# Two edits of a two-layer diffusion backbone: square sums of 512 tokens moved to TensorE, final scalings re-ordered behind evictions and roots

## The chip, the cores and the metric

The kernel runs on one core of one Trainium2 chip, as a single launch. The metric is the device time of that launch in microseconds (us). Each core has five engines with instruction queues of their own, worked off in order: TensorE (PE, matmuls into PSUM), VectorE (DVE), ScalarE (ACT), GpSimd (POOL) and SyncE (SP, which here only issues DMAs). [...]

## The reference, cut to what matters

The program is a backbone of two layers over 1024 latent tokens and a prefix of 256 context tokens, all with 1024 features, in float32. Layer 0 mixes tokens by two groups of attention heads (A: global, B: within 128 tokens, with a sink), layer 1 by a convolution (C) and by attention over a 2-D neighbourhood (D). Before each layer the stream is normalised, and the output is a last normalisation of the latent stream:

```python
def rms_norm(x, g):
    xf = x.astype(jnp.float32)
    y = xf * lax.rsqrt(jnp.mean(xf * xf, axis=-1, keepdims=True) + EPS)
    return (y * g.astype(jnp.float32)).astype(x.dtype)
...
    for i in range(DEPTH):
        ...
        h_lat = rms_norm(x_lat, norm_g[i]) * (1.0 + sc_l[:, None, :]) + sh_l[:, None, :]
        h_ctx = rms_norm(x_ctx, norm_g[i]) * (1.0 + sc_c) + sh_c
        ...
        x_lat = x_lat + g_l[:, None, :] * y_lat
        ...
    return rms_norm(x_lat, final_g)
```

So each normalisation needs, for every token, the sum of the squares of its 1024 features, then a root, then a scaling of all features. The change touches two of these: the one that opens layer 1, for the middle 512 of the 1280 tokens, and the last one.

## The kernel before

Features lie on the 128 partitions, in 8 slices `e` (or `dk`), and tokens along the free axis, in three chunks: chunk 0 is the 256 context tokens, chunks 1 and 2 are 512 latent tokens each. A float32 product is made of three matmuls on split operands (`mm3`, L345 to L347: high by high, low by high, high by low); the split of a tile into a high part (a cast on ACT) and a low part (a subtraction on POOL or DVE) is the helper `split` (L325, L328).

**Layer 0** runs attention in 40 groups (4 head groups by 10 blocks of 128 queries). A group goes through up to 10 tiles of keys. For each tile PE makes scores `st` (L522, L526; two PSUM banks), ACT the exponential `pf` (L534) and its high part `ph`, POOL the low part `pl` (L328), and three tiles later PE adds `ov` (L473 to L475; one bank). At a group's end DVE transposes and inverts the sums (L483 to L486) and scales (`y`, L683, L685). A group's maxima for the shift are found two groups ahead: PE makes scores once more into `mx` (L633, L645; two banks), DVE reduces each (`mp`, L635, L646) and all of them to `nmt` (L429); PE transposes that (`trn`, L450), and DVE writes it into `QL` (L451), without which the group's scores can't be finished.

Other work is woven between: generators `main` (attention) and `fill` are advanced in turns, and a scheduler that knows priorities then sets each engine's order. Beside the last head group the fill is `final_proj(1)` and `norm_h(1)`: for each slice `e` the output projection of chunk 1 (`po` on PE), the eviction with residual (`x`, DVE, L967), the square (ACT, L992 and L998) and its addition into one accumulator `acc` (L1000; DVE for even `e`, POOL for odd). The squares from the second on share a single buffer, `sq1` with `bufs=1`. Then `rstd_steps` sums `acc` over partitions on PE (`trs`, L262), takes the root with a power on POOL (L247) and a Newton step on DVE (L248 to L250), and spreads it (`bc`, L273); `make_h` scales the eight slices on DVE (L335) and splits them (ACT L338, L341; DVE L339; POOL L328). Chunk 2 and chunk 0 follow once attention is done.

**The end of the program** normalises three pieces, `k` = 0 (512 tokens), 1 and 2 (256 each), in the order `EVS = "e1 a1 e2 b1 a2 f0 f1 b2 f2"`: `e` is the last projection with its evictions (L1440), squares (L1470) and sums (`sum4`, L280: four squares at once, each into its own 32 partitions of a bank `pb`), `a` and `b` are the two halves of the root (`roots` keeps for each root the DVE instruction that starts it, the POOL power and the last Newton instruction), and `f` is the scaling `final_norm`: for the slices in `FNP[k]` on ACT and POOL (L1494, L1498), for the others on DVE (L1508). After every second slice SP issues a DMA to the output (L1510). `tc.issue_after(ins)` pins the instructions of a block behind `ins`, but only those that run on the engine of `ins`; the rest of the block gets no such edge.

## Time and profile before

| what | us |
|---|---|
| median of 3 runs (lowest, highest) | 1542.24 (1541.05, 1546.29) |
| the profiled execution, whole | 1542.41 |
| its span, first to last instruction | 1540.6 |
| PE, DVE, ACT, POOL busy in the span | 1457.2, 1042.5, 746.1, 793.3 |

Times in the profile count from the start of the span. The last head group with the work woven beside it runs from about 840 to 918, and the end of the program (the pieces 1 and 2) from about 1510 to 1540.6. A row of the timeline gives start, duration, engine, line, operation, tiles and count, and in brackets how long the engine was idle before and what ended that. PEclk is the share of its full clock that TensorE was granted.

### The profile page before, as it was taken

The numbers are of one execution on the slowest core, as the hardware profiler recorded it, in microseconds if no ns is written. First come the engines' busy times: TensorE is split into PE (matmuls) and PEld (weight loads), VectorE is DVE, ScalarE is ACT, GpSimd is POOL, SyncE is SP. The second block draws the span as 40 slices with busy tenths as digits, with TensorE's granted clock in tenths as the row PEclk, the third lists the DMA queues.
The fourth block names the chain that finished last, engine by engine and source line by source line (L and its number), as shares of the span: only waits on it lengthen the run. The fifth ranks groups of instructions, "written<-read, shape, count | busy, mean of one in ns | idle before, by whom it ended". The sixth has DMA issues, their size and how long they took to land.

```text
span 1540.6 us, 21500 instructions
## 1 busy us (share of the span) xinstructions
PE 1457.2 (95%) x7112; PEld 1171.6 (76%) x7112; DVE 1042.5 (68%) x2106; ACT 746.1 (48%) x1416; POOL 793.3 (51%) x631
## 2 busy tenths in 40 slices
PE   6899999998998999999999889999999999989996
PEld 2776888796896777886776558888887788868875
DVE  2833466479678956556667948999938675567866
ACT  3721434444444455447546665443434455455564
POOL 3440335446355757557646665665533434364664
PEclk7899999999999999999999889999999999999998
DMA  9474315423312236121111112211484677877642
GB/s 367 151 243 145 103 62 175 147 64 93 120 56 71 89 124 225 52 69 53 42 43 58 44 33 79 59 56 41 141 258 143 204 214 225 261 225 235 186 125 109
DMA packets 154168, 199.83 MB, mean 130 GB/s; under 512 B 14717, under 2 KB 95817, under 8 KB 154057
## 3 DMA queue, kind: packets, MB, share of 16 engines
q1 hardware_dynamic: 147392, 186.88, 38.6%
q10 hardware_dynamic: 6664, 11.57, 2.2%
q8 instruction: 56, 0.92, 0.3%
q14 instruction: 56, 0.45, 0.1%
HBM read 148.07 MB, written 49.02 MB: 128 GB/s over the span
## 4 chain that ended last, share of the span: by engine, by line
PE 76%; DVE 12%; DMA 5%; issue 3%; POOL 2%; ACT 2%; SPq 0%; DVEq 0%; POOLq 0%; ACTq 0%
PE p L345 6%; PE p L346 6%; PE p L347 6%; PE ov L473 4%; PE ov L475 4%; PE ov L474 4%; PE po L345 4%; PE po L347 4%; PE po L346 4%; PE st L522 4%; PE st L526 4%; PE pq L345 3%; PE pq L346 3%; PE pq L347 3%; PE pg L345 2%
## 5 line engine op out<-in xcount | busy, mean ns | idle before, releaser
L328 POOL TENSOR_TENSOR pl<-pf,ph 128x512 fp32r<-128x512 f32 (+4 forms) x321 | 395.3, 1243 | 369.2 <-ACT ph L325 305.8
L534 ACT ACTIVATE pf<-st 128x512 f32<-128x512 f32 x284 | 166.3, 597 | 199.3 <-PE st L526 160.8
L328 POOL TENSOR_TENSOR wl<-wr,wh 128x512 fp32r<-128x512 f32 (+2 forms) x131 | 171.0, 1317 | 145.9 <-ACT wh L325 131.5
L325 ACT CAST ph<-pf 128x512 fp32r<-128x512 f32 (+4 forms) x364 | 209.4, 588 | 28.2 <-PE ov L474 17.9
L345 PE MATMUL p<-hh,wh 128*128 128x512 f32 x448 | 176.2, 394 | 3.1 <-DVE spq L1166 1.4
L346 PE MATMUL p<-hl,wh 128*128 128x512 f32 x448 | 174.5, 390 | 0.0
L347 PE MATMUL p<-hh,wl 128*128 128x512 f32 x448 | 173.0, 391 | 0.0
L522 PE MATMUL st<-QH,KAt 128*128 128x512 f32 (+4 forms) x364 | 141.7, 390 | 6.9 <-ACT pf L534 6.0
L473 PE MATMUL ov<-ph,Vt 128*128 128x512 f32 (+4 forms) x364 | 140.8, 387 | 3.8 <-DVE y L683 2.0
L475 PE MATMUL ov<-pl,Vt 128*128 128x512 f32 (+4 forms) x364 | 141.0, 387 | 2.1 <-POOL pl L328 2.0
L474 PE MATMUL ov<-ph,Vt 128*64 128x512 f32 (+4 forms) x364 | 138.9, 382 | 0.0
L526 PE MATMUL st<-QL,KBt 68*128 68x512 f32 (+4 forms) x364 | 136.5, 386 | 0.9 <-issue 0.8
L325 ACT CAST wh<-wr 128x512 fp32r<-128x512 f32 (+2 forms) x134 | 81.0, 612 | 96.3 <-PE p L346 18.7
L1110 DVE SCALAR_TENSOR_TENSOR cps<-U,taps,cps 128x512 f32<-128x512 f32 x184 | 125.9, 749 | 0.7
L345 PEld LDWEIGHTS p<-hh,wh 128*128 128x128 f32 x448 | 84.2, 188 | 21.2 <-ACT wh L325 1.8
L347 PEld LDWEIGHTS p<-hh,wl 128*128 128x128 f32 x448 | 84.1, 188 | 17.5
L346 PEld LDWEIGHTS p<-hl,wh 128*128 128x128 f32 x448 | 84.2, 188 | 16.8 <-issue 0.2
L646 DVE TENSOR_REDUCE mp<-mx 128x1 f32<-128x512 f32 x128 | 85.2, 680 | 17.2 <-PE mx L645 16.3
L345 PE MATMUL pq<-wh,hh 128*128 128x384 f32 x256 | 88.0, 344 | 2.8 <-ACT hh L325 2.8
L967 DVE SCALAR_TENSOR_TENSOR x<-po,modT,x 128x512 f32<-128x512 f32 (+1 forms) x72 | 47.0, 657 | 63.2 <-PE po L347 62.8
L522 PEld LDWEIGHTS st<-QH,KAt 128*128 128x128 f32 x364 | 70.0, 193 | 24.4 <-ACT pf L534 9.1
L475 PEld LDWEIGHTS ov<-pl,Vt 128*128 128x128 f32 x364 | 70.1, 193 | 22.4 <-POOL pl L328 5.0
(283 smaller groups left out, 3473.8 us busy)
## 6 DMA issues: line engine op xcount, KB each, us to landing
mw<-in_mod_w_dram SPq DMA_DIRECT2D x16, 1024.0 KB, 5.5
Q<-qs SPq DMA_DIRECT2D x40, 256.0 KB, 2.2
QH<-Q SPq DMA_DIRECT2D x80, 128.0 KB, 2.7
mw<-in_mod_w_dram SPq DMA_DIRECT2D x16, 512.0 KB, 6.5
wr<-in_od_d_dram SPq DMA_DIRECT2D x32, 256.0 KB, 3.2
wr<-in_ev_qkv_dram SPq DMA_DIRECT2D x16, 384.0 KB, 5.2
KAt<-KD SPq DMA_DIRECT2D x16, 384.0 KB, 6.5
wr<-in_od_wo_dram SPq DMA_DIRECT2D x22, 256.0 KB, 3.4
```

What stands on the lines that cost most here:

```text
L325: acts.append(SC.copy(hi, src))
L328: (GP if leng == "g" else VE).tensor_tensor(lo, src, hi.bitcast(F32), op=ALU.subtract)
L345: PE.matmul(o, lh, rh, start=first, stop=False)
L346: PE.matmul(o, lh, rl, start=False, stop=False)
L347: last.append(PE.matmul(o, ll, rh, start=False, stop=end))
L473: PE.matmul(o, V[:, 64:192], ph[:, :n], start=(t == 0), stop=False)
L474: PE.matmul(g.ov[0:64, q0 : q0 + n], V[:, 0:64], ph[:, :n], start=False, stop=False)
L475: PE.matmul(o, V[:, 64:192], pl[:, :n], start=False, stop=(last and g.sink is None))
L522: sts.append(PE.matmul(st[:, :n], KA[:, cs], g.QH[:, q0 : q0 + n], start=True, stop=False))
L526: PE.matmul(st[:, :n], KB[0:68, cs], g.QL[0:68, q0 : q0 + n], start=False, stop=True)
L534: acts.append(SC.activation(pf[:, :n], st[:, :n], AF.Exp, scale=1.0 if g.bias else SCALE))
L1110: VE.scalar_tensor_tensor(pc, uc, w, pc, op0=ALU.mult, op1=ALU.add)
```

## The change

Four things are edited:

1. Chunk 1's squares are no longer added on DVE and POOL. Eight squares (L997 of the changed kernel) go into three `sq1` buffers and, for every fourth, the `acc1` buffer; after the fourth and the eighth, `sum4` adds four of them on PE into a bank `pb`, and ACT copies the bank to `acc` (L1004). The factor 1/32 undoes that each partition of `pb` holds 32 equal rows.
2. The buffers of `sq1` grow from one to three, for chunk 0 too.
3. DVE's scalings of piece 0 are pinned anew: slice 1, which had no pin, behind the last evictions; slice 3, which stood behind these, behind the root of piece 1, as slices 5 and 7 do.
4. POOL's scalings of pieces 1 and 2 are pinned to another instruction of the last root: not to its power on POOL but to its last Newton step, which runs on DVE.

```diff
             na = 2 if c == 2 else 1
             pool, tag, bufs = (kvp, "QH", 3) if c == 2 else (op_, "acc1", 1)
-            accs[c] = [pool.tile([P, 512], F32, tag=tag, name=nm("acc1"), bufs=bufs)[:, :n] for _ in range(na)]
+            def acc1():
+                return pool.tile([P, 512], F32, tag=tag, name=nm("acc1"), bufs=bufs)[:, :n]
+
+            accs[c] = [] if c == 1 else [acc1() for _ in range(na)]
+            sqs = []
             for e in range(DK):
                 yield from out0(final, e, c, *ws[e // 2])
                 if c > 0:
                     SY.dma_start(X1[:, e, t0 - 256 : t0 - 256 + n], x1[c][:, e, :])
-                if e < na:
+                if c == 1:
+                    sqs.append(op_.tile([P, 512], F32, tag="sq1" if e % 4 < 3 else "acc1", name=nm("sq1"), bufs=3 if e % 4 < 3 else 1))
+                    SC.activation(sqs[-1], x1[c][:, e, :], AF.Square)
+                    if e == 0:
+                        pb = bank("tr", nm("pb"))
+                    if e % 4 == 3:
+                        sum4(pb, sqs[-4:], n, e // 4)
+                    if e == 7:
+                        accs[c].append(acc1())
+                        SC.copy(accs[c][0], pb)
+                elif e < na:
                     SC.activation(accs[c][e], x1[c][:, e, :], AF.Square)
                 else:
                     if c < 2:
-                        sq = op_.tile([P, 512], F32, tag="sq1", name=nm("sq1"), bufs=1)
+                        sq = op_.tile([P, 512], F32, tag="sq1", name=nm("sq1"), bufs=3)
...
-            bc = yield from rstd_steps(op_, accs[c], n, "pp", tr="pp")
+            bc = yield from rstd_steps(op_, accs[c], n, "pp", 1.0 / 32.0 if c == 1 else 1.0, tr="pp")
...
                         if k == 1:
-                            cx.enter_context(tc.issue_after(roots[-1][1].ins))
+                            cx.enter_context(tc.issue_after(roots[-1][2].ins))
                         GP.tensor_tensor(x, x, bcs, op=ALU.mult)
                 else:
                     with ExitStack() as cx:
                         pins = []
-                        if k == 0 and e > 1:
-                            pins = adds[-DK:] + ([roots[-2][2]] if e > 3 else [])
+                        if k == 0:
+                            pins = [roots[-2][2]] if e > 1 else adds[-DK:]
                         elif k == 1:
                             pins = [roots[-1][0 if e < 3 else 2]]
```

The engines' orders differ between the two kernels in these two places only. Three pieces follow; numbers behind names tell buffers apart.

ACT beside the last head group, before (a row is an instruction, in the engine's order; `sq_2319` is the square of the last slice):

```order
L534 ACTIVATE pf_8611<-st_8606 128x512
L325 CAST hh_7170<-y_8563 128x2x128
L998 ACTIVATE sq_2307_9117<-x_1776_7151 128x512
L325 CAST ph_8609<-pf_8611 128x512
L534 ACTIVATE pf_8667<-st_8662 128x512
L325 CAST ph_8665<-pf_8667 128x512
L998 ACTIVATE sq_2319_9156<-x_1776_7151 128x512
L534 ACTIVATE pf_8697<-st_8692 128x512
L534 ACTIVATE pf_8734<-st_8729 128x512
```

and in the changed kernel:

```order
L325 CAST hh_7170<-y_8563 128x2x128
L997 ACTIVATE sq_2308_9117<-x_1776_7151 128x512
L997 ACTIVATE sq_2320_9155<-x_1776_7151 128x512
L534 ACTIVATE pf_8611<-st_8606 128x512
L534 ACTIVATE pf_8667<-st_8662 128x512
L325 CAST ph_8609<-pf_8611 128x512
L325 CAST ph_8665<-pf_8667 128x512
L1004 COPY acc_2321_9161<-pb_8872 128x512
L534 ACTIVATE pf_8697<-st_8692 128x512
```

The last square stood behind three tiles' worth of attention work and right ahead of two exponentials; now the last two squares stand ahead of all of these, and the copy of the sum stands where the square was.

PE at the same place in the changed kernel, the first sum of four and what stands around it (the second sum's four matmuls stand together, behind the maxima `mx_8505` and ahead of the scores `st_8692`):

```order
L347 MATMUL po_9036<-hh_7149,wl_8818 128x512
L280 MATMUL pb_8872<-sq_2274_8995,one 32x512
L280 MATMUL pb_8872<-sq_2236_8870,one 32x512
L280 MATMUL pb_8872<-sq_2252_8922,one 32x512
L522 MATMUL st_8580<-QH_8177,KAt_554 128x512
L633 MATMUL mx_8470<-KAt_554,QH_8449 128x256 x2
L526 MATMUL st_8536<-QL_8178,KBt_549 128x512
L645 MATMUL mx_8474<-KAt_554,QH_8449 128x512
L526 MATMUL st_8580<-QL_8178,KBt_549 128x512
L280 MATMUL pb_8872<-sq_2264_8960,one 32x512
L345 MATMUL po_9071<-hh_7149,wh_8823 128x512
```

Three of the four matmuls of the first sum stand together and the fourth apart. On DVE, the order around `make_h` before:

```order
L429 TENSOR_REDUCE nmt_8534<-mp_8465 128x4
L248 TENSOR_TENSOR nt_9167<-nr_9166,rbv_9164 128x4
L249 SCALAR_TENSOR_TENSOR nt_9167<-nt_9167,nr_9166 128x4
L250 SCALAR_TENSOR_TENSOR nr_9166<-nt_9167,nr_9166 128x4
L328 TENSOR_TENSOR hc_7129<-y_8633,hc_7129 128x2x128
L328 TENSOR_TENSOR pl_8733<-pf_8734,ph_8732 128x512
L451 TENSOR_TENSOR QL_8450<-trn_8569,k_bd 4x512
L635 TENSOR_REDUCE mp_8639<-mx_8640 128x2
L335 SCALAR_TENSOR_TENSOR x_1776_7151<-x_1776_7151,gs_105,bc_9220 128x512 x8
```

and in the changed kernel:

```order
L646 TENSOR_REDUCE mp_8465<-mx_8514 128x1
L646 TENSOR_REDUCE mp_8465<-mx_8517 128x1
L335 SCALAR_TENSOR_TENSOR x_1776_7151<-x_1776_7151,gs_105,bc_9224 128x512 x8
L646 TENSOR_REDUCE mp_8465<-mx_8531 128x1
L339 SCALAR_TENSOR_TENSOR hl_9230<-x_1776_7151,modT_103,hh_9229 128x512
L429 TENSOR_REDUCE nmt_8534<-mp_8465 128x4
L339 SCALAR_TENSOR_TENSOR hl_9230<-x_1776_7151,modT_103,hh_9229 128x512
L451 TENSOR_TENSOR QL_8450<-trn_8569,k_bd 4x512
L635 TENSOR_REDUCE mp_8639<-mx_8640 128x2
```

`nmt` and `QL` of the last group but one stood ahead of the eight scalings L335; now they stand behind these and behind two splits.

POOL at the very end, before (`nr` are the powers of the roots of pieces 0, 1 and 2; `x` are scalings):

```order
L247 TENSOR_TENSOR nr_15574<-rbv_15572,mhalf 128x4
L1498 TENSOR_TENSOR x_3240_13686<-x_3240_13686,bcs_15756 128x512 x4
L247 TENSOR_TENSOR nr_15669<-rbv_15667,mhalf 128x2
L247 TENSOR_TENSOR nr_15750<-rbv_15748,mhalf 128x2
L1498 TENSOR_TENSOR x_3242_13688<-x_3242_13688,bcs_15774 128x256 x2
L1498 TENSOR_TENSOR x_3242_13688<-x_3242_13688,bcs_15793 128x256 x2
```

and in the changed kernel:

```order
L247 TENSOR_TENSOR nr_15578<-rbv_15576,mhalf 128x4
L1512 TENSOR_TENSOR x_3242_13690<-x_3242_13690,bcs_15760 128x512 x4
L247 TENSOR_TENSOR nr_15673<-rbv_15671,mhalf 128x2
L1512 TENSOR_TENSOR x_3244_13692<-x_3244_13692,bcs_15778 128x256 x2
L247 TENSOR_TENSOR nr_15754<-rbv_15752,mhalf 128x2
L1512 TENSOR_TENSOR x_3244_13692<-x_3244_13692,bcs_15797 128x256 x2
```

The two scalings of piece 1 now stand ahead of the last root's power, not behind it. On DVE the scaling of slice 1 of piece 0 moved from ahead of the sixteen evictions L1440 to behind them, and that of slice 3 from behind them to behind the Newton step of piece 1's root.

## The prediction

> **What bounds the kernel now.** I read the page's first part first, to see which engine sets the whole:
>
> ```profile
> PE 1457.2 (95%) x7112; PEld 1171.6 (76%) x7112; DVE 1042.5 (68%) x2106; ACT 746.1 (48%) x1416; POOL 793.3 (51%) x631
> ```
>
> TensorE is busy 95% of the span. Work taken off another engine is therefore worth only what TensorE loses by waiting for it, or at a lowered clock. So I went next to the two places that the orders show as changed, with busy time by stretches of 5 or 10 us (columns: length, then PE, PEld, DVE, ACT, POOL busy with counts, granted clock, DMA share, GB/s):
>
> ```profile
> 840.00:850.00 10.00, 10.00 (x48) 8.04 (x47) 6.72 (x13) 5.24 (x10) 7.50 (x6) 1.00 0.55 184
> ...
> 855.00:860.00 5.00, 2.41 (x11) 1.52 (x9) 4.96 (x7) 2.76 (x6) 3.40 (x3) 1.00 0.33 116
> 860.00:865.00 5.00, 4.45 (x15) 3.63 (x16) 4.20 (x10) 0.98 (x3) 1.27 (x1) 0.59 0.00 0
> 865.00:870.00 5.00, 5.00 (x19) 3.52 (x19) 4.08 (x10) 2.80 (x6) 2.31 (x2) 0.72 0.09 26
> ...
> 875.00:880.00 5.00, 3.23 (x10) 1.27 (x9) 5.00 (x8) 5.00 (x10) 4.29 (x4) 1.00 0.00 0
> 880.00:885.00 5.00, 2.97 (x7) 1.58 (x8) 5.00 (x6) 3.11 (x6) 5.00 (x4) 0.64 0.00 0
> 885.00:890.00 5.00, 4.45 (x10) 2.45 (x10) 4.82 (x12) 3.03 (x6) 3.88 (x4) 0.50 0.00 0
> ```
>
> Up to 850 TensorE is full; then it is not the bound. It starves twice, at 857 and from 876 on, and after each the granted clock is low. The timeline of each engine tells why the first stall comes (DVE, POOL, ACT, then PE):
>
> ```profile
> 854.47 0.74 DVE L967 SCALAR_TENSOR_TENSOR x<-po,modT,x 128x512 f32<-128x512 f32 x1
> ...
> 856.32 1.36 DVE L328 TENSOR_TENSOR hl<-y,hh 128x256 fp32r<-128x256 f32 x1
> 857.60 1.75 DVE L1000 TENSOR_TENSOR acc<-acc,sq 128x512 f32<-128x512 f32 x1
> ...
> 860.09 1.27 POOL L1000 TENSOR_TENSOR acc<-acc,sq 128x512 f32<-128x512 f32 x1 [1.29 <-ACT sq L998]
> ...
> 859.38 0.63 ACT L998 ACTIVATE sq<-x 128x512 f32<-128x512 f32 x1 [2.21 <-DVE acc L1000]
> 859.92 1.07 ACT L534 ACTIVATE pf<-st 128x512 f32<-128x512 f32 x2
> ...
> 860.55 0.50 PE L522 MATMUL st<-QH,KAt 128*128 128x512 f32 x1 [3.14 <-ACT pf L534]
> ...
> 865.68 0.63 PE L474 MATMUL ov<-ph,Vt 128*64 128x512 f32 x1
> 866.10 0.63 PE L475 MATMUL ov<-pl,Vt 128*128 128x512 f32 x1
> ...
> 868.02 0.40 PE L474 MATMUL ov<-ph,Vt 128*64 128x512 f32 x1
> 868.25 0.40 PE L475 MATMUL ov<-pl,Vt 128*128 128x512 f32 x1
> ```
>
> It is one chain. The last square has to wait for the one `sq1` buffer, which DVE's addition (1.75 us) holds until 859.35. ACT works in order, so the two exponentials behind the square wait with it, and TensorE waits 3.14 us for a score bank. From start to start a matmul then takes 0.42 us (865.68 to 866.10) and later 0.23 (868.02 to 868.25).
>
> **Part 1, the squares of chunk 1.** Three additions leave DVE, four leave POOL; none of that counts by itself, since neither bounds TensorE elsewhere in the stretch. What counts:
>
> *The stall.* The squares now hold four buffers that PE frees, and stand early in ACT's order. The last eviction (now at 854.47) moves back by some 1.9 us, because two of the three groups of new matmuls stand ahead of its projection (0.9 each, below), to 856.4; eviction and square (0.74 and 0.63) end at 857.8, half a microsecond behind the point at which PE stops now, and PE itself comes later by the same matmuls. So nothing is left to wait for. Gain 3.1 us; if the new wait for that square takes half of it, 1.5.
>
> *The half clock behind it.* The clock columns 0.59 and 0.72 mean half speed for 4.1 and 2.8 us, 6.9 together, in which PE always had work. At 0.42 us where 0.23 would do, 45% of it is lost: 3.1 us. Bounds 0 and 3.1.
>
> [...]
>
> *The new matmuls.* The trace has `sum4` with 256 columns:
>
> ```profile
> 1522.77 0.64 PE L280 MATMUL pb<-sq,one 128*32 128x256 f32 x8
> 1523.34 0.39 PE L345 MATMUL po<-od,wh 128*128 128x256 f32 x1
> ```
>
> Four of them (eight records) keep the next matmul off for 0.57 us. With 512 columns twice that, 1.14 us, is the most for four together. The first sum stands as three and one, so there are three such groups: cost at most 3.4 us, at least 1.1 (two groups that don't grow with the columns). I take 0.9 each, 2.7, near the upper end, because PE is full there (the row of 840). The copy of the bank on ACT (0.6 us, as long as the square) lies beside these.
>
> *The second starved stretch.* Its rows, DVE and then PE:
>
> ```profile
> 869.49 0.68 DVE L451 TENSOR_TENSOR QL<-trn,k_bd 4x512 fp32r<-4x512 f32 x1 [0.17 <-PE trn L450]
> ...
> 871.07 5.36 DVE L335 SCALAR_TENSOR_TENSOR x<-x,gs,bc 128x512 f32<-128x512 f32 x8 [0.18 <-PE bc L273]
> ...
> 881.15 2.84 DVE L339 SCALAR_TENSOR_TENSOR hl<-x,modT,hh 128x512 fp32r<-128x512 f32 x2
> ...
> 884.65 0.80 PE L645 MATMUL mx<-KAt,QH 128*128 128x512 f32 x1 [1.38 <-DVE mp L646]
> ...
> 888.93 0.77 PE L473 MATMUL ov<-ph,Vt 128*128 128x512 f32 x1 [0.36 <-DVE y L683]
> ...
> 918.02 0.74 PE L345 MATMUL po<-hh,wh 128*128 128x512 f32 x2 [3.51 <-ACT hh L325]
> ```
>
> Between 875 and 890 PE idles 1.77 + 2.03 + 0.55 = 4.35 us, waiting for DVE, which is full with `make_h` (5.36 us of L335, then the L339) and has the maxima between. The half clock lasts 3.6 us of the second and all of the third row; about 7 of these 8.6 us are work, and 45% of that is 3.1. Lost there: about 7.5 us. `make_h` does not shrink, so most of it stays: in the new order PE waits for an exponential behind L341, for `nmt` behind the L335, for `QL` and for the `ov` bank, by these durations some 4.7 us, with two slow windows. But the maxima now stand between other work, and all four L339 are done before the last six are wanted. I take a gain of 1.5; bounds 4.5 and a loss of 3.2 (two more slow windows at 45% of 3.4).
>
> Sum of part 1: -3.1 - 3.1 + 2.7 - 1.5 = -5.0. After 918 the two kernels' orders agree but for some rows of chunk 0's norm, behind PE's full work,
>
> ```profile
> 925.00:930.00 5.00, 5.00 (x24) 4.14 (x23) 4.21 (x7) 2.94 (x5) 2.99 (x2) 1.00 0.83 281
> ```
>
> so a lead at 918 should reach the end.
>
> **Part 2, the last 25 us.** The rows on PE, DVE and POOL:
>
> ```profile
> 1518.75 0.41 PE L347 MATMUL po<-od,wl 128*128 128x256 f32 x1
> ...
> 1518.60 1.87 DVE L1508 SCALAR_TENSOR_TENSOR x<-x,fg,bcs 128x512 f32<-128x512 f32 x1 [0.75 <-ACT bcs L1490]
> 1520.39 3.21 DVE L1440 SCALAR_TENSOR_TENSOR x<-po,modT,x 128x256 f32<-128x256 f32 x8
> ...
> 1520.92 0.39 PE L345 MATMUL po<-od,wh 128*128 128x256 f32 x1 [0.75 <-DVE x L1440]
> ...
> 1528.13 0.74 DVE L1508 SCALAR_TENSOR_TENSOR x<-x,fg,bcs 128x512 f32<-128x512 f32 x1
> 1528.79 0.15 DVE L248 TENSOR_TENSOR nt<-nr,rbv 128x2 f32<-128x2 f32 x1
> ...
> 1530.81 0.70 POOL L247 TENSOR_TENSOR nr<-rbv,mhalf 128x2 f32<-128x2 f32 x1 [2.21 <-DVE rbv L265]
> 1531.47 1.41 POOL L1498 TENSOR_TENSOR x<-x,bcs 128x256 f32<-128x256 f32 x2
> ...
> 1531.54 0.67 DVE L248 TENSOR_TENSOR nt<-nr,rbv 128x2 f32<-128x2 f32 x1
> ```
>
> The scaling that leaves the head of the line took 1.87 us beside POOL's scalings (0.74 at 1528.13, without these). The evictions can then start when their projections end, the first at 1519.2 (1518.75 + 0.41) and not at 1520.4: 1.2 us earlier, and the squares and sums with them. Half of it is given back at the last root: a third scaling (0.7 us) now stands ahead of its start on DVE, and POOL's two scalings (1.41 us) ahead of its power. In exchange the Newton steps no longer run beside these (0.67 us at 1531.54 for what took 0.15 at 1528.79). Chain by chain: last root 0.6 us earlier.
>
> The end is not the root, however, but the output:
>
> ```profile
> 1520.53 17.12 SPq L1510 DMA_DIRECT2D out_dram<-x  x12
> ...
> 1530.00:1535.00 5.00, 1.57 (x10) 1.18 (x8) 4.90 (x12) 0.75 (x2) 2.38 (x4) 0.83 1.04 394
> 1535.00:1539.00 4.00, 0.00 (x0) 0.00 (x0) 2.09 (x6) 0.00 (x0) 1.10 (x2) 0.50 1.09 384
> ```
>
> The DMA engines are full from 1530 to 1539 at 390 GB/s. In the old kernel the first 0.52 MB left at 1520.53, in idle time. Now slice 1 is ready only behind the last eviction: its scaling, at 1528.13 for the slice that stands there now, comes 1.2 us earlier and ends at 1527.6. So all 4.2 MB (1024 by 1024 numbers) queue up: 10.7 us at this rate from about 1528.5 on, which ends at 1539.2, against 1539.4 now. Part 2 brings 0.3 us, bounds 0.9 and a loss of 0.8.
>
> **The sum** is made against the profiled execution, 1542.41, which is 0.17 above the median: 1542.4 - 5.0 - 0.3 = **1537.1**.
>
> **The rivals.** *The gain is swallowed (1540.1).* The first stall goes, but PE merely reaches the next wait sooner: the second stretch gets one slow window more (45% of 3.4, 1.5 us) where I have a gain: -3.5 + 1.5 - 0.3. For it: PE's order has `trn` behind `nmt`, and `nmt` now stands behind the L335. Against: the maxima that held PE up at 884.65 are spread out.
>
> *The half clock is worth one slow window (1538.7).* The 6.9 us at half speed belong to one execution; where they are 3.4, the term is 1.5. [...] Against: the two rows above.
>
> *Slower (1549.2).* The last two groups set the pace from the moment at which `QL` is there. Now that is at 870.2, ahead of L335. In the new order L335 starts 3.5 us (the sum's first three terms) earlier than at 871.07 and ends at 873.0; a maximum (0.6), two L339 (1.4 each), `nmt` (0.2) and `QL` itself (0.7) follow, to 877.3. If the 47.8 us from `QL` to 918.0 stay, the stage ends 7.1 later: 1542.4 + 7.1 - 0.3. It decides if PE has nothing else to do while it waits. Against: PE has had `QL` since 870.2 and starved for the maxima until 890 all the same.
>
> *The end does not do what it says (1538.2).* POOL's scalings of piece 1 are not behind the last root but ahead of its power. If that root then comes as late as now, or later by one scaling (0.7), part 2 is a loss of 0.8: 1542.4 - 5.0 + 0.8. It changes little, as part 1 is the larger by far.
>
> *The second stretch nearly goes (1532.5).* It gains 6 of its 7.5 us: 1542.4 - 3.5 - 6.1 - 0.3.
>
> **How the numbers follow.** Chances: forecast 0.42, swallowed 0.26, one window 0.07, slower 0.07, end 0.08, nearly gone 0.10. A change of 0.3% is 4.6 us, about what a measurement of this kernel can tell: below 1537.6 is faster, above 1546.9 slower. The forecast's own range, by its bounds, is 1534 to 1539.5, and I put 0.37 of its 0.42 below 1537.6; with all of the last case and 0.05 from the scatter of the others faster gets 0.52, slower 0.06, the same 0.42. The range for 8 in 10 reaches from between the last case and the forecast, 1533.3, past the swallowed gain to 1541.7.
>
> **What would show it.** Right: no wait of PE for `pf` of 3 us near 857 and a clock of 1.0 from 860 to 867; L280 with 512 columns at about 1 us for four; the row 918.02 five us earlier. At the end, the first eviction of piece 1 at a distance of 1.2 us less from the end of `bc`, and the DMA engines full for 10.7 us without a gap. Wrong: PE idle or slow between 866 and 885 for longer than 8 us in all, or the matmuls of a sum waiting for their square.

## The result, and the profile after

The changed kernel takes 1537.17 us (median of 12 runs, 1535.27 to 1541.50), the kernel before in the same session 1544.59 us (12 runs, 1540.57 to 1552.09). The ratio is 0.9958, 95% interval 0.9945 to 0.9971: by it 6.5 us less, with 4.5 to 8.5 in the interval. The forecast was 1537.1, by 5.3 us less (0.34%). The same two kernels in a later session gave 0.9975 (0.9960 to 0.9989), 3.9 us less. The profiled run of the changed kernel took 1540.89 us (span 1539.1), one of its slower ones.

Stretches of 5 us of the changed kernel around the changed place (length, then PE, PEld, DVE, ACT, POOL busy with counts, granted clock, DMA share, GB/s):

```profile
855.00:860.00 5.00, 5.00 (x26) 3.13 (x25) 4.48 (x11) 3.37 (x7) 1.27 (x3) 1.00 0.27 105
860.00:865.00 5.00, 5.00 (x28) 4.02 (x27) 3.99 (x8) 2.53 (x5) 3.67 (x4) 1.00 0.09 26
865.00:870.00 5.00, 5.00 (x27) 3.86 (x26) 5.00 (x9) 4.12 (x8) 2.56 (x2) 1.00 0.00 2
870.00:875.00 5.00, 1.78 (x6) 0.66 (x5) 4.55 (x8) 5.00 (x10) 4.35 (x4) 0.88 0.00 0
875.00:880.00 5.00, 3.97 (x11) 2.88 (x12) 4.94 (x7) 3.10 (x6) 2.66 (x3) 0.50 0.00 0
880.00:885.00 5.00, 4.09 (x15) 2.50 (x14) 4.12 (x10) 3.77 (x8) 4.87 (x5) 0.93 0.00 0
```

The hole at 857 and the half clock behind it are gone: TensorE is full at clock 1.00 up to 870. The second hole is still there, only earlier, from 870.5. The timeline of TensorE shows both, with the price of the sums (DVE rows last):

```profile
848.58 1.06 PE L280 MATMUL pb<-sq,one 128*32 128x512 f32 x6
850.94 1.04 PE L280 MATMUL pb<-sq,one 128*32 128x512 f32 x2
857.63 1.07 PE L280 MATMUL pb<-sq,one 128*32 128x512 f32 x8
860.14 0.95 PE L262 MATMUL trs<-ones,acc 128*128 128x2 f32 x8
872.12 0.51 PE L522 MATMUL st<-QH,KAt 128*128 128x512 f32 x1 [1.63 <-ACT pf L534]
874.95 0.38 PE L450 MATMUL trn<-ident,nmt 128*4 128x128 f32 x1 [1.59 <-DVE nmt L429]
877.27 0.80 PE L633 MATMUL mx<-KAt,QH 128*128 128x256 f32 x2 [1.03 <-DVE QL L451]
898.37 0.47 PE L473 MATMUL ov<-ph,Vt 128*128 128x512 f32 x1 [1.21 <-DVE y L683]
914.79 2.07 PE L345 MATMUL po<-hh,wh 128*128 128x512 f32 x4 [3.50 <-ACT hh L325]
...
840.11 0.17 DVE L429 TENSOR_REDUCE nmt<-mp 128x4 fp32r<-128x12 f32 x1
866.84 5.35 DVE L335 SCALAR_TENSOR_TENSOR x<-x,gs,bc 128x512 f32<-128x512 f32 x8
```

Two rows serve as marks from here on. The last `nmt` before the change (840.11 here, 840.78 in the profile of before) is the start: up to there the engines' orders are the same, but for one row each on ACT and POOL. The row `po<-hh` behind the wait of 3.50 us (914.79 here, 918.02 before) is the **exit** of layer 0's attention. `L335` of chunk 1 lies between. Measured from the start, `L335` begins at 26.73 in place of 30.29, the exit comes at 74.68 in place of 77.24. A lead of 3.6 us at `L335` is 2.6 us at the exit.

The tail of the changed kernel, on DVE, POOL and the output queue:

```profile
1517.19 1.76 DVE L1454 SCALAR_TENSOR_TENSOR x<-po,modT,x 128x256 f32<-128x256 f32 x4 [1.36 <-PE po L347]
...
1526.56 2.07 DVE L1522 SCALAR_TENSOR_TENSOR x<-x,fg,bcs 128x512 f32<-128x512 f32 x3
1528.55 0.15 DVE L265 TENSOR_SCALAR rbv<-trs 128x2 f32<-128x2 f32 x1
...
1527.95 1.94 POOL L1512 TENSOR_TENSOR x<-x,bcs 128x256 f32<-128x256 f32 x2 [2.05 <-ACT bcs L1504]
1529.86 0.69 POOL L247 TENSOR_TENSOR nr<-rbv,mhalf 128x2 f32<-128x2 f32 x1
...
1526.24 9.61 SPq L1524 DMA_DIRECT2D out_dram<-x  x12
```

The first eviction comes earlier, but the last `rbv` waits behind three scalings, and POOL's power (L247) stands behind POOL's scalings: 1.3 us pass between `rbv` and it. The first output leaves at 1526.24, and from 1527 to 1538 the DMA engines are full (the last two numbers of the row are their share and GB/s):

```profile
1527.00:1538.00 11.00, 2.04 (x12) 1.65 (x11) 6.96 (x19) 0.80 (x3) 4.00 (x5) 0.60 1.03 381
```

### The profile page after: what moved, and what is told of

It reads as the page before. It is cut to its first block, busy times and chain, and to the rows that moved or that the text cites. A ratio compares the mean times of both kernels' runs of the same rounds, so it can differ in the third digit from the quotient of the medians.

```text
span 1539.1 us, 21527 instructions
## 1 busy us (share of the span) xinstructions
PE 1455.1 (95%) x7128; PEld 1169.7 (76%) x7128; DVE 1036.8 (67%) x2103; ACT 746.2 (48%) x1417; POOL 785.5 (51%) x627
## 4 chain that ended last, share of the span: by engine, by line
PE 80%; DVE 9%; issue 4%; DMA 2%; POOL 2%; ACT 2%; SPq 0%; DVEq 0%; POOLq 0%; ACTq 0%
PE p L345 6%; PE p L347 6%; PE p L346 6%; PE ov L473 5%; PE ov L475 4%; PE ov L474 4%; PE po L345 4%; PE po L346 4%; PE po L347 4%; PE st L522 4%; PE st L526 4%; PE pq L345 3%; PE pq L347 3%; PE pq L346 3%; PE pg L345 2%
## 5 line engine op out<-in xcount | busy, mean ns | idle before, releaser
L328 POOL TENSOR_TENSOR pl<-pf,ph 128x512 fp32r<-128x512 f32 (+4 forms) x321 | 393.9, 1239 | 380.3 <-ACT ph L325 323.6
L328 POOL TENSOR_TENSOR wl<-wr,wh 128x512 fp32r<-128x512 f32 (+2 forms) x131 | 169.5, 1304 | 144.6 <-ACT wh L325 130.3
L325 ACT CAST ph<-pf 128x512 fp32r<-128x512 f32 (+4 forms) x364 | 209.0, 588 | 22.8 <-PE ov L474 10.7
```

What stands on the lines that cost most here:

```text
L325: acts.append(SC.copy(hi, src))
L328: (GP if leng == "g" else VE).tensor_tensor(lo, src, hi.bitcast(F32), op=ALU.subtract)
```

## The experiments

Single profiles of one kernel differ by some microseconds, so the places are compared by distances inside each profile. All of them in one table (us; start, `L335` and exit as above; "first eviction" is that of piece 1, counted like "tail" from the start of the `rbv` of piece 0, the tail up to the end of the span; the ratio is to the kernel before, with its 95% interval):

| kernel | start to `L335` | `L335` to exit | start to exit | first eviction behind `rbv` | tail | ratio, 95% |
|---|---|---|---|---|---|---|
| before | 30.29 | 46.95 | 77.24 | 7.73 | 27.93 | |
| e2_tail (layer 0 as before) | 31.70 | 47.61 | 79.31 | 6.54 | 28.03 | 0.9993, 0.9978 to 1.0008 |
| e3_bufs | 29.35 | 47.42 | 76.77 | 7.82 | 28.11 | 0.9995, 0.9984 to 1.0006 |
| e5_fill | 28.94 | 49.57 | 78.51 | 7.85 | 28.14 | 0.9996, 0.9983 to 1.0009 |
| the change | 26.73 | 47.95 | 74.68 | 6.54 | 28.46 | 0.9958, 0.9945 to 0.9971 |
| e7_again (the change) | 26.74 | 48.17 | 74.91 | 6.74 | 28.15 | 0.9975, 0.9960 to 0.9989 |
| e1_layer0 | 26.73 | 48.26 | 74.99 | 7.73 | 27.93 | 0.9982, 0.9969 to 0.9994 |
| e4_pin | 26.74 | 48.25 | 74.99 | 6.54 | 28.23 | 0.9972, 0.9960 to 0.9983 |
| e6_nmt | 26.73 | 50.20 | 76.93 | 6.54 | 28.55 | 0.9998, 0.9985 to 1.0012 |
| e8_warm | 26.73 | 48.24 | 74.97 | 6.53 | 27.95 | 0.9983, 0.9966 to 0.9999 |
| e9_hold | | | 65.75 | 6.54 | 28.80 | 0.9944, 0.9922 to 0.9967 |
| e10_tailwarm | 26.73 | 48.28 | 75.01 | 5.79 | 27.10 | 0.9970, 0.9955 to 0.9984 |
| e11_pldve | 26.73 | 45.98 | 72.71 | 6.63 | 29.51 | 0.9967, 0.9949 to 0.9985 |
| e12_both | | | 67.19 | 5.79 | 27.80 | 0.9937, 0.9914 to 0.9960 |

### Each part alone

**e1_layer0**: the old pins of the final scalings, the new sums.

```diff
-                            cx.enter_context(tc.issue_after(roots[-1][2].ins))
+                            cx.enter_context(tc.issue_after(roots[-1][1].ins))
...
-                        if k == 0:
-                            pins = [roots[-2][2]] if e > 1 else adds[-DK:]
+                        if k == 0 and e > 1:
+                            pins = adds[-DK:] + ([roots[-2][2]] if e > 3 else [])
```

> Only the part in layer 0 (sums of chunk 1's squares on TensorE), with the old order of the final scalings. Theory of the prediction: nearly the whole gain is here, 5.0 us less than the kernel before, and 0.3 us more than the changed kernel. Rival (the tail hides a loss of 0.6 us, as its trace hints): 7 us less than before, so a little faster than the changed kernel. Rival (the tail brings more than was thought, since the whole change brought 6.5 us by the timed runs): 5 us less than before and 1.5 us more than the changed kernel. In the trace all three want no 3 us wait of TensorE near 857.

Measured: 0.9982, 2.8 us less than before (0.9 to 4.8); the 5.0 of the theory lies just outside. **e2_tail** is the other half: these pins, the old sums.

> Only the order of the final scalings, with the old sums in layer 0. Theory of the prediction: 0.3 us less than before, between 0.9 less and 0.8 more, so no difference that can be measured; its trace keeps the 3.1 us wait near 857. Rival (the end does not do what it says): 0.6 us more. Rival (the tail brings more than was thought): 1.5 us less.

Measured: 0.9993, 1.1 us less, with 0 well inside the interval. By time, then, the gain is in layer 0 and the tail cannot be told from nothing; which of the three theories on the tail holds, the ratios don't settle (e1_layer0 lies below the changed kernel's 3.9 to 6.5 us, which would speak for a tail that brings something). The distances show no gain: the old tail takes 28.03 us on average (before, e3_bufs, e5_fill, e1_layer0; 27.93 to 28.14), the new one 28.23 (e2_tail, the two profiles of the change, e6_nmt, e8_warm; 27.95 to 28.55). That is 0.2 us more, but the two ranges overlap. In e9_hold and e11_pldve, whose TensorE order in the tail is another, it is longer still.

e2_tail brought more than was asked of it: a second profile of the old layer 0.

```profile
862.14 0.79 PE L522 MATMUL st<-QH,KAt 128*128 128x512 f32 x1 [3.13 <-ACT pf L534]
```

```profile
860.00:865.00 5.00, 2.86 (x8) 2.24 (x8) 4.87 (x9) 1.60 (x3) 1.66 (x2) 0.69 0.00 0
865.00:870.00 5.00, 5.00 (x18) 3.91 (x17) 3.50 (x11) 1.50 (x3) 2.12 (x2) 0.50 0.01 4
870.00:875.00 5.00, 5.00 (x24) 3.82 (x23) 3.38 (x6) 2.42 (x6) 2.70 (x3) 0.78 0.08 24
```

The stall is the same to 0.01 us, but the half clock behind it lasts 10.2 us, not 6.8. (The shortest stretch of half clock in the profile of before lasts 3.41 us, as at 806.31; that length is called a slow window here, so 6.8 us are two of them and 10.2 three.) So the same code has `L335` at 30.29 in one run and at 31.70 in the next, and what the change takes away is 3.6 us from the one and 5.0 us from the other.

### Is the single buffer the cause of the stall?

**e3_bufs**, on the kernel before:

```diff
-                        sq = op_.tile([P, 512], F32, tag="sq1", name=nm("sq1"), bufs=1)
+                        sq = op_.tile([P, 512], F32, tag="sq1", name=nm("sq1"), bufs=3)
```

> The kernel before, with three buffers for the squares in place of one; the additions stay on VectorE and GpSimd, nothing is added to TensorE. If the single buffer is what makes the stall (the prediction's chain), the stall of 3.1 us and the 3.1 us of half clock behind it go without the 2.7 us of new matmuls: some 6 us less than before, about as fast as the changed kernel or faster. Rival (VectorE and GpSimd are too full for these additions, whatever the buffers: the running sum is late and with it the norm, and the second starved stretch gets longer): 2 us less at most, and a wait of TensorE for the running sum or for nmt that is longer than before.

Measured: 0.9995, no difference. What is left of the stall, and the clock:

```profile
856.65 0.50 PE L522 MATMUL st<-QH,KAt 128*128 128x512 f32 x1 [0.52 <-ACT pf L534]
857.96 0.50 PE L645 MATMUL mx<-KAt,QH 128*128 128x512 f32 x1 [0.57 <-DVE mp L646]
```

```profile
855.00:860.00 5.00, 3.75 (x17) 2.68 (x18) 4.85 (x11) 1.92 (x4) 3.96 (x4) 0.94 0.11 41
860.00:865.00 5.00, 4.65 (x12) 2.90 (x11) 4.10 (x11) 1.92 (x4) 1.97 (x2) 0.50 0.09 26
```

The long stall goes, so the buffer was its cause: that half of the theory stands. But two waits of 0.5 us remain, the first of the two at the old place and the other for a maximum that DVE's additions hold up, and 6.8 us of half clock came with them. `L335` comes 0.9 to 2.4 us earlier, and nothing of it is seen in the time. The rival (VectorE and GpSimd are too full for the additions, 2 us at most) told the outcome. The buffers alone, then, bring nothing that the time shows; the gain of the change comes only with the sums on TensorE.

### What does the half clock cost?

**e5_fill**: the kernel before, with useless matmuls at the place of its stall.

```diff
...
+                if len(sts) == 228:
+                    dm = bank("tr", nm("dm"))
+                    with tc.issue_after(sts[-1].ins):
+                        for _ in range(12):
+                            d = PE.matmul(dm[:, :n], KA[:, cs], g.QH[:, q0 : q0 + n], start=True, stop=True)
+                    cx.enter_context(tc.issue_after(d.ins))
...
```

> The kernel before, with twelve useless matmuls (512 columns, into a free bank that nobody reads) on TensorE at the place of its 3.14 us wait. The wait for the exponential stays as long as it was, only the idle time is filled. Theory of the prediction (the pause lowers the clock, and 6.9 us at half speed cost 3.1 us): clock 1.00 from 860 to 867, L335 of chunk 1 starts 27.2 us behind the nmt of 840.78 (30.3 in the profile of before), 3.1 us less than the kernel before. Rival (one slow window at most belongs to the pause): 1.5 us less. Rival (the low clock has another cause than the pause): the clock falls all the same, 0 us. The rows behind L335 are put in another order by this edit, so the time of the whole can be off by about 1 us more.

Measured: 0.9996. On TensorE, and the stretch behind it:

```profile
852.70 2.90 PE L527 MATMUL dm<-QH,KAt 128*128 128x512 f32 x12
856.03 0.50 PE L529 MATMUL st<-QH,KAt 128*128 128x512 f32 x1 [0.43 <-ACT pf L541]
```

```profile
855.00:860.00 5.00, 4.48 (x23) 3.07 (x21) 4.84 (x11) 2.30 (x5) 1.28 (x1) 1.00 0.00 0
860.00:865.00 5.00, 4.42 (x24) 3.22 (x23) 3.48 (x9) 2.18 (x5) 2.27 (x2) 1.00 0.09 26
```

The score matmul leaves at the same distance from the start as before (19.80 against 19.77 us), so the exponential was as late as ever; only the idle time is filled, and the clock stays at 1.00 from 855 to 870 (in before it is 0.59 and 0.72 in the two stretches from 860 to 870). That settles the cause at this place: with the idle time the half clock went. The price, from start to `L335`: 28.94 against 30.29 and 31.70, so 1.4 to 2.8 us (`bc` stands two rows later in this order, which may hide some of it). The theory wanted 27.2, 3.1 us less than the profile of before; in size the rival's 1.5 is the nearer, though two slow windows went and not one. The whole kernel gained nothing, as the rows behind `L335` were reordered and the second stretch had five slow windows there, 17.1 us.

**e8_warm** does the same for the wait of 3.50 us at the exit, which all kernels have; `fin_mm` holds the last `ov` matmul with its two operands.

```diff
...
-        run(final_proj(2))
+        f2 = final_proj(2)
+        dm = bank("tr", nm("dm"))
+        with tc.issue_after(fin_mm[0].ins):
+            for _ in range(13):
+                d = PE.matmul(dm, fin_mm[2][:, 64:192], fin_mm[1], start=True, stop=True)
+        with tc.issue_after(d.ins):
+            next(f2)
+        run(f2)
```

> The changed kernel with thirteen useless matmuls (512 columns, into a free bank) on TensorE in its wait of 3.50 us for hh (before 914.79), which both kernels have. Theory (idle time of TensorE lowers the clock, wherever it comes from): the wait stays, no half clock from 914 to 920 (3.4 to 6.8 us of it in five profiles), 1.5 to 3.0 us less than the changed kernel up to the middle norms. Rival (the clock falls also behind a full TensorE): no gain. The edit moves rows in layer 1 too, which may add or take some microseconds in the whole time; the trace between 905 and 935 decides.

```profile
910.52 3.13 PE L1036 MATMUL dm<-ph,Vt 128*128 128x512 f32 x13
914.20 1.21 PE L346 MATMUL po<-hh,wh 128*128 128x512 f32 x4 [0.54 <-ACT hh L326]
...
930.10 1.95 PE L263 MATMUL trs<-ones,acc 128*128 128x2 f32 x16 [1.82 <-DVE acc L1015]
```

The clock stays at 1.00 from 909 to 919 (0.66 in the changed kernel from 914 to 919), as expected, and it was worth nothing: TensorE now reaches `trs` early and waits 1.82 us for the running sum. The `rbv` of chunk 2 comes 92.9 us behind the start, against 92.3 and 92.5 in the profiles of the change and up to 93.6 in others of the same order (e1_layer0, e4_pin, e10_tailwarm). Ratio 0.9983, with layer 1 in another order, so no gain in the time either. So the half clock at 860, where TensorE was the bound, cost 1.4 to 2.8 us (e5_fill), and the one at 914, where it was not, nothing that was seen.

### What holds the second stretch?

Of the lead of 3.6 to 5.0 us at `L335`, about 0.9 is lost on the way to the exit: 48.2 us in four profiles of the new order (47.95, 48.26, 48.25, 48.17) against 46.95 and 47.61 in two of the old. **e6_nmt** tests the first suspect, that `nmt` and `QL` now stand behind all eight `L335`. (`nmts` and `qls` collect the instructions L429 and L451; `[-2]` is the last group but one.)

```diff
...
+                if l == 1 and c == 1 and dk >= 3:
+                    cx.enter_context(tc.issue_after((nmts[-2] if dk < 5 else qls[-2]).ins))
                 VE.scalar_tensor_tensor(x, x, gs[l][:, dk, cond : cond + 1], bc, op0=ALU.mult, op1=ALU.mult)
```

> The changed kernel with two pins: the fourth and fifth L335 of chunk 1 stand behind nmt on VectorE, the last three behind QL; so nmt and QL no longer stand behind all eight. Theory (the second stretch lost its gain because L335, now earlier, holds up nmt and QL): the waits of 1.59 us for nmt and 1.03 us for QL go, the exit of the stage (the matmul po<-hh at 914.79) comes 2 us or more earlier against the nmt of 840.11, and the kernel takes 2 us less than the changed one. Rival (the exit is set by the exponentials and POOL's L328, which are full from 901 to 911): the waits go, but the exit moves by less than 0.5 us, and the time by 0 to 0.5 us.

```profile
868.70 0.17 DVE L434 TENSOR_REDUCE nmt<-mp 128x4 fp32r<-128x12 f32 x1
870.21 0.68 DVE L456 TENSOR_TENSOR QL<-trn,k_bd 4x512 fp32r<-4x512 f32 x1
```

```profile
881.60 1.39 PE L650 MATMUL mx<-KAt,QH 128*128 128x512 f32 x2 [1.79 <-DVE mp L651]
916.21 2.07 PE L350 MATMUL po<-hh,wh 128*128 128x512 f32 x4 [3.50 <-ACT hh L325]
```

`nmt` comes 29.4 us behind the start (34.6 in the change), the waits for it and for `QL` are gone, and the exit is 2.0 us **later**, 76.93; the gain in time is gone too (0.9998). The theory falls, and the rival's "less than 0.5 us" was still too kind. A wait that is removed came back as one for a maximum (1.79 us), with 13.6 us of half clock from 873 on. The waits named on TensorE were not what held the stretch.

**e9_hold** takes the other suspect away: `make_h` of chunk 1 waits until the attention is done (`dones` holds the last group's L685 on DVE).

```diff
...
+            if c == 1:
+                yield
             h1[c] = new_h(c)
-            make_h(1, c, lambda dk: x1[c][:, dk, :], bc[:, :n], h1[c])
+            with tc.issue_after(dones[-1].ins) if c == 1 else ExitStack():
+                make_h(1, c, lambda dk: x1[c][:, dk, :], bc[:, :n], h1[c])
...
-        weave(main, NSTEP[U1 // 2] - GL - O1[0] - O1[1] - O1[2], fill, O1[3])
+        weave(main, NSTEP[U1 // 2] - GL - O1[0] - O1[1] - O1[2], fill, O1[3], all_fill=False)
+        run(fill)
```

> The changed kernel with make_h of chunk 1 held back until the last attention group of layer 0 is done (its first scaling stands behind that group's last DVE row), so that the second starved stretch has none of its work. Theory (make_h's work on VectorE and ScalarE, about 11 us on VectorE and 8 us on ScalarE, is what starves TensorE there and sets the end of the stretch): the waits of 1.63, 1.59 and 1.03 us go and the exit of the layer's attention (po<-hh at 914.79, 74.7 to 75.0 us behind the nmt at 840) comes 4 us or more earlier. Rival (the group's own chain of exponentials and L328 on GpSimd sets the exit): the waits go, but the exit moves by less than 1.5 us. The whole time is no gain in either case, as the same work comes later, in front of layer 1.

```profile
870.00:875.00 5.00, 4.43 (x22) 3.22 (x20) 4.15 (x7) 3.01 (x6) 3.59 (x4) 1.00 0.00 0
875.00:880.00 5.00, 4.35 (x17) 2.94 (x18) 4.32 (x11) 4.25 (x9) 4.26 (x4) 1.00 0.00 0
880.00:885.00 5.00, 5.00 (x24) 3.78 (x22) 3.30 (x6) 3.91 (x7) 3.21 (x3) 1.00 0.10 30
```

```profile
905.51 1.65 PE L345 MATMUL po<-hh,wh 128*128 128x512 f32 x3 [3.50 <-ACT hh L325]
```

The starved stretch is gone. The first slow window begins at 903.69, in the wait before the exit, and the exit comes at 65.75 in place of 74.9: 9.1 us earlier, twice the "4 us or more". (In e12_both, which has the same edit, a slow window falls at 892 and the exit comes at 67.19, 7.7 us earlier.) So it was `make_h`'s work itself, on DVE, ACT and POOL beside the exponentials; that no order of it could have given much is likely but not shown, as e6_nmt tried only one. That this kernel is also faster as a whole was not expected: ratio 0.9944 (5 runs), 8.6 us less than before and by its middle value less than the change, though the intervals overlap. Its price comes back: counted from the start mark, the lead over the change's profile is 2.0 us at the `rbv` of chunk 2 and 1.5 at the first `nmt` of layer 1 (1195.06 there). Then it rises to 6.6 at the `rbv` of piece 0. That rise lies in layer 1, whose order moved with this edit: between these two marks it takes 310.6 us here and 310.8 in e12_both, and 312.4 to 315.6 in five profiles of the change's order (the change, e7_again, e1_layer0, e4_pin, e10_tailwarm). Which of its rows brought it is open.

**e11_pldve** gives DVE the last ten `L328` (pl) of the attention.

```diff
-            split(pf[:, :n], ph[:, :n], pl[:, :n], "s", "v" if cnt[0] % vshare == 0 else "g")
+            split(pf[:, :n], ph[:, :n], pl[:, :n], "s", "v" if cnt[0] % vshare == 0 or (layer[0] == 0 and len(sts) > 241) else "g")
```

> The changed kernel with the last ten L328 (pl) of layer 0's attention on VectorE (idle there) in place of GpSimd. In the profile of the changed kernel GpSimd runs seven of them back to back for 1.32 us each from 900.79 to 910, ScalarE's pair (exponential and cast) takes 1.22 us. Theory (GpSimd sets the pace of the last exponentials): the exit po<-hh comes 1 us earlier, 73.9 us behind the nmt at 840 in place of 74.9. Rival (ScalarE sets the pace): 0.3 us or less. The order in layer 1 changes too, so only the stretch up to the exit tells it apart.

```profile
910.91 2.07 PE L345 MATMUL po<-hh,wh 128*128 128x512 f32 x4 [3.50 <-ACT hh L325]
```

The exit comes at 72.71, 2.2 us earlier, twice what the theory gave. GpSimd sets the pace of the last exponentials, where DVE stands idle. With e9_hold this says that from `L335` to the exit the work of DVE, ACT and POOL sets the pace, and TensorE follows. Ratio 0.9967; layer 1 has another order here too.

### The tail

**e4_pin**: GpSimd's pin back on the power, which is a GpSimd instruction.

```diff
-                            cx.enter_context(tc.issue_after(roots[-1][2].ins))
+                            cx.enter_context(tc.issue_after(roots[-1][1].ins))
```

> The changed kernel with GpSimd's scalings of piece 1 tied to the power of the last root again, which stands on GpSimd, in place of the last Newton step, which does not. The power then starts right behind its input, about 1.3 us earlier than at 1529.86 in the changed kernel's profile. Theory (the output transfers, full from the first issue on, set the end): 0.0 to 0.3 us less than the changed kernel. Rival (the last root sets the end): 1.3 us less.

The last `rbv` ends at 1525.63, POOL's power and the output queue follow:

```profile
1525.71 0.70 POOL L247 TENSOR_TENSOR nr<-rbv,mhalf 128x2 f32<-128x2 f32 x1 [2.87 <-DVE rbv L265]
...
1523.18 9.32 SPq L1524 DMA_DIRECT2D out_dram<-x  x12
```

The power starts at once, 0.23 us behind the start of `rbv` and not 1.31. The root gains little by it (it ends 20.18 us behind the `rbv` of piece 0, in the change 20.48 and 20.19), since its Newton steps now run beside POOL's scalings and take 0.67 us in place of 0.16. The tail is 0.23 us shorter than in the one profile of the change and 0.08 longer than in the other, and the ratio of 0.9972 lies between the two of the change. As the root itself hardly moved, this run does not separate the two theories. The output queue does: from the first output to the end it is 12.85 to 12.87 us in nine of the ten profiles with the new order of DVE's scalings (13.67 in e11_pldve), and in the change the DMA engines are full for 10.76 us of these, without a gap. So the transfers set the end, counted from the moment at which the first slice is ready.

**e10_tailwarm** fills TensorE's wait of 2.85 us for the root of piece 0. The useless matmuls stand behind the last `ov` matmul and ahead of `bc` of piece 0, which for that is written behind the attention in the program; one square on ScalarE is pinned behind the copy of a bank, so that the copy keeps its place.

```diff
         bc = bank(tag, nm("bc"))
...
+            if warm:
+                with tc.issue_after(fin_mm[0].ins):
+                    for _ in range(11):
+                        d = PE.matmul(bc, fin_mm[2][:, 64:192], fin_mm[1], start=True, stop=True)
+                cx.enter_context(tc.issue_after(d.ins))
...
```

> The changed kernel with eleven useless matmuls in TensorE's wait of 2.85 us before the last bc of piece 0 (at 1513.79), ahead of bc on TensorE, so that the clock does not fall in the tail; the rest of the order stays but for two rows on ScalarE and one projection. Theory (the half clock of 6.8 us that nearly every profile shows from 1512 on slows bc and the twelve projections that the first evictions wait for): clock 1.00 from 1512 to 1519, first eviction of piece 1 2.0 us behind the last Newton step (L250, nr) in place of 3.4, and the kernel 1.0 to 1.5 us faster than the changed one. Rival (the end is set by the output transfers): the evictions come earlier, the end does not, 0 to 0.3 us.

```profile
1513.00:1516.00 3.00, 2.51 (x15) 1.79 (x15) 2.21 (x7) 1.06 (x2) 0.00 (x0) 1.00 0.00 0
1516.00:1519.00 3.00, 3.00 (x23) 2.75 (x22) 2.40 (x7) 1.78 (x6) 2.78 (x3) 1.00 0.00 0
```

The clock stays at 1.00 (in the change 0.50 and 0.51 in the same two stretches). The first eviction comes 5.79 us behind `rbv` in place of 6.54 to 6.74, 0.8 us earlier and not 1.4, since the projections now wait for `od`, the split output of layer 1's attention. The first output leaves 14.24 us behind `rbv` in place of 15.30 and 15.59, and the end follows: the tail takes 27.10 us in place of 28.15 and 28.46, 1.0 to 1.4 less, the theory's size. In the time (0.9970) a microsecond is not to be seen.

**e7_again** is the change itself.

> The changed kernel itself, word for word, beside the kernel before and the others of this call. From its own timed runs: 6.5 us less than before (ratio 0.9958). From the parts measured alone (layer 0 2.8 us, tail 1.1 us): 3.9 us less (0.9975). The traces so far put layer 0 at 2.3 to 4.3 us and the tail at 0 to a loss of 0.5 us: 3 us less (0.998).

0.9975: the middle of the three expectations.

**e12_both** joins e9_hold and the filled wait of e10_tailwarm, without that run's pin on ScalarE.

> The changed kernel with both edits that helped: make_h of chunk 1 held back until the attention of layer 0 is done, and eleven useless matmuls in TensorE's wait before the last bc of piece 0. If the two are independent, the gains add: 8.6 us (held back, ratio 0.9944) and a further 1.2 us in the tail (the distance from the last rbv of piece 0 to the end 27.1 us in place of 28.2 to 28.5), so 9.8 us less than the kernel before, ratio 0.9936, and 4 to 6 us less than the changed kernel. Rival (the held-back kernel's gain in layer 1 came from another phase of the clock's windows and not from its order): 5 to 6 us less than before, ratio 0.9965.

0.9937 (6 runs), 9.7 us less than before, as the sum said (0.9936); the rival's 0.9965 lies just outside the interval (0.9914 to 0.9960). The tail is 27.80 us against 28.80 in e9_hold. It is the fastest kernel of this study by its middle value; its interval and that of e9_hold overlap almost wholly.

## Why the prediction was right, and where it was not

The time was forecast at 5.3 us less; two sessions gave 6.5 and 3.9. The parts behind it:

- *The stall, 3.1.* Right, in place and size: 3.14 and 3.13 us in two profiles of the old code, none in ten of the new.
- *The half clock behind it, 3.1.* Right in cause (e5_fill), and inside its bounds, but taken at the upper one: 1.4 us measured against the profile that the prediction was made with (6.8 us of half clock), 2.8 against the other (10.2 us). The size of the half clock is no constant of the stall: it is two slow windows in the one profile and three in the other. Where the prediction counts a slow window as 3.4 us, the traces have 3.41 (806.31 in before).
- *The new matmuls, 2.7.* Right: each of the three groups holds the next matmul off for 0.97 to 0.99 us, 2.95 in all. The lone matmul costs as much as the four together.
- *The sum of these at `L335`, 3.5 us earlier.* 3.56 against the profile that it was made with, 5.0 against the other. But the parts as measured alone don't add up to it: 3.14 + 1.4 - 2.95 is 1.6 us. Some 2 us come from elsewhere, and no run isolates them. The additions that left DVE and POOL, which the prediction put at nothing ("none of that counts by itself"), are a candidate; the rows that may hide part of the price in e5_fill are another. That the sum came out to the tenth is partly luck.
- *The second starved stretch, a gain of 1.5.* **Wrong.** `L335` to exit takes 0.9 us more. The step that failed is "the maxima now stand between other work, and all four L339 are done before the last six are wanted": it looked for what TensorE waits for, as if a wait that is moved out of the way were time won. e6_nmt moved them further and lost 2 us more; e9_hold shows that `make_h`'s work is what the stretch pays for. The loss is near what the rival "the gain is swallowed" had at this place (1.5).
- *The tail, a gain of 0.3.* Not seen, inside its bounds: 0.2 us longer on average, with overlapping ranges. The first eviction is 1.2 us earlier as forecast (7.73 to 6.54 behind `rbv`; 6.74 in the second profile), and the transfers take 10.76 us without a gap, as forecast (10.7). What was mis-sized is their start: 16.5 and 16.2 us behind the `rbv` of piece 0, where 1528.5 is 15.8. "Last root 0.6 us earlier" was too much as well: it ends 20.48 us behind that `rbv` in four old tails and 20.26 in five new ones, 0.2 earlier, as three scalings stand ahead of the last `rbv` on DVE. The rival on the power's place was right in mechanism: POOL's scalings do run first and put the power off by 1.08 us (1.31 behind `rbv`, 0.23 in e4_pin).

At the exit the new order leads the profile that the prediction was made with by 2.3 us, and the other profile of the old layer 0 by 4.4 (77.24 and 79.31 against 74.9). Against the first, the rival "the gain is swallowed" fits the trace better than the forecast; the timed 3.9 to 6.5 us lie nearer to the second. So the forecast met the time partly by luck: the profile it was made with had the shorter half clock behind the stall, which makes the first sum small by 1.4 us, and it made the gain of the second stretch 2.4 too large. Of the prediction's own signs, the missing stall, the full clock from 860 to 867, the price of the sums, the first eviction and the gapless transfers came as it said. The exit came 3.2 us earlier on the profile's clock and not five, and one sign of being wrong was seen as well: from 866 to 885 TensorE was idle or slow for 9.8 us, where it allowed 8.

The slower rival was right on its pieces (`L335` at 867.6 forecast, 866.84 measured; end of `QL` 877.3 and 877.22) and wrong that they decide: e6_nmt has `QL` 5.5 us earlier and the exit later.

## What to carry to other kernels

Before a wait is removed, ask which engines are full behind it: where DVE, ACT and POOL carry the pace, the wait that TensorE shows is only the place where it stands. There, taking work out of the stretch (9.1 and 7.7 us at the exit, some of which comes back later) was worth more than either order of it that was tried. A pause of TensorE cost more than its length where TensorE was the bound next (the one of 3.14 us a further 1.4 to 2.8 us, e5_fill), and nothing was seen of it at the exit (e8_warm: `rbv` 92.9 us behind the start against 92.3 and 92.5); in the tail, useless matmuls in an unavoidable wait were a cheap cure (1.0 to 1.4 us, e10_tailwarm). And where one profile is compared with one, do it by distances inside each, from a mark that both have.

## What the runs showed of the hardware

**The half clock, as the traces have it.** In the profiles of before and of the change 19 stretches of half clock begin between 60 and 1505 us: 14 last 3.41 us, four 6.83 and one 10.24. In each of the two their starts lie whole multiples of 3.41 us apart, and the offset is another: counted from the start of the span, 0.77 us are left over in before and 0.03 in the change.

**Pauses of TensorE and the clock.** At three places the half clock went when the pause was filled: at 857 (3.14 us of pause and 6.83 us of half clock from 860.92 in before; 1.00 from 855 to 870 in e5_fill), at the exit (3.50 us, and 3.41 us of half clock from 914.80, in the change; 1.00 from 909 to 919 in e8_warm) and in the tail (2.85 us, and 6.83 us of half clock from 1512.13, in the change; 1.00 from 1510 to 1519 in e10_tailwarm). In e3_bufs 6.8 us of half clock came with two waits of 0.52 and 0.57 us. Which pauses lower the clock, and for how long, no run isolates. The eight `trs` matmuls of chunk 1 take 1.70 us at half clock (863.12 in before) and 0.95 at full clock (860.14 in the change).

**The scatter between profiles.** The mean granted clock is 0.971 (before) to 0.979 (e9_hold) over a whole run, 66 to 89 us of half clock. The start mark lies at 836.2 to 843.4 us in the 14 profiles, and the half clock ahead of it (27.3 to 41.0 us) does not fix it: it is 27.3 us both at 838.2, e11_pldve, and at 839.8, e9_hold. What else moves the mark is open.
